# A two-layer decoder trunk on one core: the two passes with high weights as one matmul of 512 columns

## The chip, the core and the metric

The kernel runs on one core of a Trainium2 chip. The metric is the device time of one execution in microseconds; before the change it is 662.47 us (median of 3 runs, 661.54 to 662.65). The core's engines are TensorE (PE in the rows, its weight loads PEld), VectorE (DVE), ScalarE (ACT), GpSimd (POOL) and SyncE (SP, which issues most of the transfers here). TensorE writes into PSUM, eight banks of 128 partitions x 512 fp32.

## The reference, cut to what matters

```python
def reference(x, ...):                       # x: (1, 256, 1024) float32
    for i in range(2):
        h = rms_norm(x, norm_mix_g[i])
        x = x + (nsa_mixer(h, ...) if i == 0 else diff_mixer(h, ...))
        h = rms_norm(x, norm_ffn_g[i])
        x = x + conv_ffn(h, ...)
    return rms_norm(x, final_norm_g)

def rms_norm(x, g):
    return x * lax.rsqrt(jnp.mean(x * x, axis=-1, keepdims=True) + EPS) * g

def diff_mixer(h, w_in, ...):
    q, k, v = split(h @ w_in)                # 8 heads, two halves of 64 each
    p = softmax(q k / 8 - slopes * dist)     # of each half, causal
    a = p[:, 0] - lam * p[:, 1]
    return (rms_norm(a @ v, subln_g) * (1.0 - lambda_init)) @ w_out

def conv_ffn(h, w_up, conv_w, conv_b, w_down):
    u = causal_conv3(h @ w_up) + conv_b      # per channel, 2 x 2816 channels
    gate, val = jnp.split(u, 2, axis=-1)
    return (jax.nn.silu(gate) * val) @ w_down
```

The first mixer (`nsa_mixer`, 16 heads, three branches of attention) is touched by the change in its output projection alone.

## The kernel before

x lies transposed in `xT`: 8 tiles of 128 channels x 256 tokens. To keep fp32 accuracy, each product runs as three matmul passes on rounded parts: the weights as `hi` and `lo`, the activations as `xhi` and `xlo`, and the passes are hi by xhi, hi by xlo and lo by xhi (`passes`, L220). With the weights stationary (`mm_b`, L224), a pass over one tile is a matmul of 128x128 weights by 256 columns, so a unit of weights (128x1024, 8 tiles) takes 8 x 3 = 24 matmuls.

The class `Stream` (L60 on) brings the weights in the order of use: SyncE issues the transfers into three raw buffers, ScalarE makes `hi` of a unit (L112), VectorE `lo` (L113). `fill` keeps some units ahead.

The norm is applied late. `split_tile` (L182) splits x times gain, without the factor of a token, as soon as a residual tile is there; `norm_stats` (L201) sums the squares by TensorE, takes the power on GpSimd, makes a diagonal `dg` on VectorE (L212), spreads it by TensorE and copies it (L217) into `rr`, the factor of each token. The results of the projections are multiplied by `rr` when they leave PSUM: L762 in the diff mixer, L960 in the feed-forward.

The four phases run as `nsa`, `ffn(0)`, `diff`, `ffn(1)`. TensorE's order is that of the program text (a manual schedule for this engine); the order of VectorE, ScalarE and GpSimd is made by the scheduler of the language from dependencies and priorities. PSUM banks come from one pool of 8 in the order of their requests.

In the feed-forward a pair p (of 22) is one unit of gate channels and one of value channels. `up(p)` (L941) does 48 matmuls into one bank, gate in its first 256 columns and value in the last. `conv(p)` (L957) takes the bank by one multiply with `rr` into `us` (VectorE, L960), then the convolution (ScalarE L965, VectorE L967 four times), silu, product, and the split into `hh` (ScalarE, L974) and `hl` (VectorE, L976). `down(p - 2)` follows up(p) on TensorE: 24 matmuls of 256 columns in layer 0 (L932), 12 of 512 in layer 1 (L912). The second layer also puts `rows(i)`, four transposes (L988), behind the pairs 3, 5, 7 and 9.

`residual` (L262) adds a bank of an output projection to `xT`, splits the tile and adds its squares to the sum. In the diff mixer `proj(h, w)` makes q and k of a head (24 matmuls), `s_scores` the scores and both softmax halves (scaled and combined at L782 and L783), `s_trans` transposes them and copies them to `dva` (L794), `s_pv` multiplies them by V (L801). Its V projection (L244) takes x as the stationary side and 512 columns of weights.

Of the kernel before, what the change touches and what calls it, by code (L numbers as in the profile page):

```python
# [10 lines left out]
F32 = mybir.dt.float32  # L11
F32R = mybir.dt.float32r
# [5 lines left out]
P = 128  # L18
T = 256
# [10 lines left out]
LOOK = 3  # L30
GW = 280
# [94 lines left out]
def trunk(ctx, tc, xin, wts, cst, kst, sel, bia, msk, bib, lam, fng, out):  # L126
# [35 lines left out]
    xhi = cp.tile([P, KT, T], F32R, name="xhi")  # L162
    xlo = cp.tile([P, KT, T], F32R, name="xlo")
# [77 lines left out]

    def mm_a1(dst, unit, cols, k, kt, q):
# [19 lines left out]
    def residual(n, st, dt, ps):  # L262
        nc.vector.tensor_tensor(xT[:, dt, :], ps, xT[:, dt, :], op=OP.add)  # L263
        split_tile(n, dt)
        sum_squares(n, st, square(n, dt)[:, 0, :], dt)

    def nsa():
        with ExitStack() as c2:
# [266 lines left out]
            oh = ohp.tile([P, 2 * KT * T], F32R, tag="sh", name="oh")  # L535
            ohi = oh[:, : KT * T].rearrange("p (k t) -> p k t", k=KT)
            olo = oh[:, KT * T :].rearrange("p (k t) -> p k t", k=KT)
# [122 lines left out]
            def oproj(dt, k0, k1):  # L660
# [3 lines left out]
                mm_b(ps[:, :T], u, ohi, olo, k0, k1)  # L664
                if k1 == KT:
                    residual(1, st, dt, ps[:, :T])
# [50 lines left out]
    def diff(st):  # L717
        with ExitStack() as c2:
# [6 lines left out]
            oh = ohp.tile([P, 2 * KT * T], F32R, tag="sh", name="doh")  # L725
            ohi = oh[:, : KT * T].rearrange("p (k t) -> p k t", k=KT)
            olo = oh[:, KT * T :].rearrange("p (k t) -> p k t", k=KT)
# [27 lines left out]
            def proj(h, w, k0, k1):  # L755
# [3 lines left out]
                mm_b(ps[:, :T], u, xhi, xlo, k0, k1)  # L759
                if k1 == KT:  # L760
                    t = at.tile([P, T], F32, tag=f"qk{w}", name=f"dqks{h}{w}", bufs=3)
                    nc.vector.tensor_tensor(t, ps[:, :T], (rneg, rr)[w], op=OP.mult)  # L762
                    qk[h, w] = t

            def s_scores(h):
# [15 lines left out]
                for q, (a, b) in enumerate(((0, P), (P, 384))):  # L781
                    nc.vector.tensor_scalar(pt[:, 1, a:b], pt[:, 1, a:b], ls[:, 1, q : q + 1], None, op0=OP.mult)  # L782
# [48 lines left out]
            def oproj(dt, k0, k1):  # L831
# [3 lines left out]
                mm_b(ps[:, :T], u, ohi, olo, k0, k1)  # L835
                if k1 == KT:
                    residual(3, st, dt, ps[:, :T])
# [44 lines left out]
    def ffn(l, st, oproj_rest, dt0):  # L882
        with ExitStack() as c2:
# [57 lines left out]
            def up(p, k0=0, k1=KT):  # L941
                if k0 == 0:
                    ups[p] = ((S.next(), S.next()), bank(f"u{l}{p}").rearrange("p (a t) -> p a t", a=2))
                units, ps = ups[p]
                for kt in range(k0, k1):
                    for b in range(2):
                        for i, (w, x) in enumerate(passes(units[b], xhi, xlo)):
                            nc.tensor.matmul(  # L948
                                ps[:, b, :],
                                w[:, kt * P : (kt + 1) * P],  # L950
                                x[:, kt, :],
# [256 lines left out]
```

## Time and profile before

| | |
|---|---|
| time, median of 3 runs | 662.47 us (661.54 to 662.65) |
| the profiled execution | 662.05 us, of which the span 660.3 us |
| TensorE busy | 639.2 us, 97% of the span |
| VectorE busy | 513.9 us, 78% |
| ScalarE busy | 415.0 us, 63% |
| GpSimd busy | 28.5 us, 4% |
| read from memory | 109.27 MB, 167 GB/s over the span |
| chain that ended last | TensorE 67% of the span, of it L948 (up) 35%, L932 and L912 (down) 10% and 9%, L233 of q and k 6% |

The page gives busy time per engine, then tenths of busy time in 40 slices of the span, then the chain of work that ended last. Busy times of matmuls overlap (one of 256 columns lasts some 280 ns from its start to its modelled end, while the next starts long before), so a pace is read from a row of matmuls in the chain, as length by count, and not from the mean of one. The same holds for short operations of VectorE in a row.

### The profile page before, as it was taken

How to read it: one execution, taken by the hardware profiler on the slowest of the kernel's cores; microseconds unless marked ns; L12 is line 12 of the kernel's file. 1: busy time of each engine (PE TensorE's matmuls, PEld its weight loads, DVE VectorE, ACT ScalarE, POOL GpSimd, SP SyncE). 2: the span in 40 equal slices, each digit the busy share in tenths (PEclk: the TensorE clock that was granted, in tenths of full speed). 3: DMA queues.
4: the chain of work that ended last, by engine and by line, in shares of the span. 5: the costliest groups of instructions: out<-in, count | busy, mean ns of one | idle time of the engine just before them, and what ended most of it. 6: DMA issues, size and time to landing. Idle time of an engine off the chain costs nothing.

```text
span 660.3 us, 12584 instructions
## 1 busy us (share of the span) xinstructions
PE 639.2 (97%) x5026; PEld 609.3 (92%) x5026; DVE 513.9 (78%) x990; ACT 415.0 (63%) x817; POOL 28.5 (4%) x40
## 2 busy tenths in 40 slices
PE   8999999999999999999999999999999999999994
PEld 7989888889999999999998998989999999999993
DVE  6999988759967777788858589855987777779674
ACT  7797988658655555566636477645666555558342
POOL 3200000000000000000002000000100000000002
PEclk9999999999999999999999999999999999999998
DMA  8977301125455555555714555621755555555301
GB/s 301 308 269 267 136 16 60 65 97 201 182 193 192 192 191 188 174 184 190 255 65 148 195 159 208 216 96 31 293 188 192 192 192 188 185 180 179 99 1 64
DMA packets 15770, 111.12 MB, mean 168 GB/s; under 512 B 1976, under 2 KB 3512, under 8 KB 5976
## 3 DMA queue, kind: packets, MB, share of 16 engines
q1 hardware_dynamic: 15120, 109.70, 46.8%
q0 software_dynamic: 448, 0.37, 0.5%
q8 instruction: 39, 0.64, 0.4%
q10 hardware_dynamic: 144, 0.26, 0.1%
q14 instruction: 19, 0.16, 0.1%
HBM read 109.27 MB, written 1.05 MB: 167 GB/s over the span
## 4 chain that ended last, share of the span: by engine, by line
PE 67%; issue 23%; DVE 5%; ACT 2%; POOL 1%; DMA 1%; SPq 0%; POOLq 0%; DVEq 0%; ACTq 0%
PE u L948 35%; PE acc L932 10%; PE acc L912 9%; PE dqk L233 6%; PE dv L244 3%; PE dop L233 2%; DVE lo L113 1%; ACT dp L260 1%; DMA xT<-xin 1%; DVE cv L967 0%; PE ds L776 0%; PE ds L775 0%; DVE xT L263 0%; PE dta L792 0%; ACT xhi L183 0%
## 5 line engine op out<-in xcount | busy, mean ns | idle before, releaser
L112 ACT CAST hi<-raw 128x1024 fp32r<-128x1024 f32 (+2 forms) x199 | 202.5, 1044 | 103.5 <-PE u L948 55.4
L113 DVE TENSOR_TENSOR lo<-raw,hi 128x1024 fp32r<-128x1024 f32 (+2 forms) x199 | 239.3, 1222 | 16.1 <-ACT hi L112 15.5
L948 PE MATMUL u<-xlo,hi 128*128 128x256 f32 x704 | 197.7, 281 | 0.9 <-DVE xlo L184 0.9
L948 PE MATMUL u<-xhi,lo 128*128 128x256 f32 x704 | 198.6, 282 | 0.0
L948 PE MATMUL u<-xhi,hi 128*128 128x256 f32 x704 | 198.5, 282 | 0.0
L948 PEld LDWEIGHTS u<-xlo,hi 128*128 128x128 f32 x704 | 132.7, 188 | 1.8 <-DVE xlo L184 1.1
L948 PEld LDWEIGHTS u<-xhi,hi 128*128 128x128 f32 x704 | 132.7, 189 | 0.8 <-ACT xhi L183 0.2
L948 PEld LDWEIGHTS u<-xhi,lo 128*128 128x128 f32 x704 | 132.5, 188 | 0.0
L967 DVE SCALAR_TENSOR_TENSOR cv<-us,cs,cv 128x255 f32<-128x255 f32 (+1 forms) x176 | 74.5, 478 | 4.2 <-ACT cv L965 3.7
L960 DVE TENSOR_TENSOR us<-u,rrs 128x512 f32<-128x512 f32 x44 | 30.3, 690 | 53.3 <-PE u L948 53.2
L965 ACT ACTIVATE cv<-us,cs 128x256 f32<-128x256 f32 x88 | 48.1, 593 | 13.4 <-DVE us L960 13.2
L932 PE MATMUL acc<-hl,hi 128*128 128x256 f32 x176 | 49.7, 283 | 1.0 <-DVE hl L976 1.0
L932 PE MATMUL acc<-hh,lo 128*128 128x256 f32 x176 | 49.7, 282 | 0.0
L932 PE MATMUL acc<-hh,hi 128*128 128x256 f32 x176 | 49.6, 282 | 0.0
L974 ACT CAST hh<-cv 128x256 fp32r<-128x256 f32 x44 | 17.8, 405 | 44.6 <-DVE cv L972 44.6
L233 PE MATMUL dqk<-xhi,hi 128*128 128x256 f32 x128 | 37.1, 290 | 0.0
L233 PE MATMUL dqk<-xhi,lo 128*128 128x256 f32 x128 | 36.0, 281 | 0.0
L233 PE MATMUL dqk<-xlo,hi 128*128 128x256 f32 x128 | 36.0, 281 | 0.0
L932 PEld LDWEIGHTS acc<-hl,hi 128*128 128x128 f32 x176 | 33.2, 189 | 1.2 <-DVE hl L976 1.2
L932 PEld LDWEIGHTS acc<-hh,hi 128*128 128x128 f32 x176 | 33.3, 189 | 0.0
L932 PEld LDWEIGHTS acc<-hh,lo 128*128 128x128 f32 x176 | 33.2, 189 | 0.0
L976 DVE TENSOR_TENSOR hl<-cv,hh 128x256 fp32r<-128x256 f32 x44 | 18.6, 424 | 16.1 <-ACT hh L974 16.1
(243 smaller groups left out, 1258.7 us busy)
## 6 DMA issues: line engine op xcount, KB each, us to landing
raw<-wts SPq DMA_DIRECT2D x40, 1536.0 KB, 6.7
raw<-wts SPq DMA_DIRECT2D x34, 1024.0 KB, 5.0
raw<-wts SPq DMA_DIRECT2D x7, 512.0 KB, 4.7
raw<-wts SPq DMA_DIRECT2D x2, 1120.0 KB, 7.5
db<-bib SPq DMA_DIRECT2D x8, 192.0 KB, 4.1
xT<-xin SPq DMA_DIRECT2D x4, 256.0 KB, 5.1
out<-z SPq DMA_DIRECT2D x3, 256.0 KB, 2.0
raw<-wts SPq DMA_DIRECT2D x2, 256.0 KB, 4.5
```

The lines of the kernel that those rows point to most:

```text
L112: nc.scalar.copy(hi[:, q], r[:, q])
L113: nc.vector.tensor_tensor(lo[:, q], r[:, q], hi[:, q].bitcast(F32), op=OP.subtract)
L233: nc.tensor.matmul(dst, w[:, kt * P : (kt + 1) * P], x[:, kt, :], start=kt == 0 and i == 0, stop=kt == KT - 1 and i == 2, skip_group_check ...
L244: nc.tensor.matmul(dst, x[:, kt, q * P : (q + 1) * P], w[:, k * cols : (k + 1) * cols], start=kt == 0 and i == 0, stop=kt == KT - 1 and i ...
L912: nc.tensor.matmul(acc[q][c // 512][:, c % 512 : c % 512 + d - c], x[:, qs], w[:, c:d], start=p == 0 and i == 0, stop=p == NPAIR - 1 and i ...
L932: nc.tensor.matmul(acc[dt // 2][:, dt % 2, :], w[:, dt * P : (dt + 1) * P], x, start=p == 0 and i == 0 and dt % 2 == 0, stop=p == NPAIR - ...
L948: nc.tensor.matmul(ps[:, b, :], w[:, kt * P : (kt + 1) * P], x[:, kt, :], start=kt == 0 and b == 0 and i == 0, stop=kt == KT - 1 and i == ...
L960: nc.vector.tensor_tensor(us, ps, rr.unsqueeze(1).to_broadcast([P, 2, T]), op=OP.mult)
L965: nc.scalar.activation(cv[:, b, :], us[:, b, :], AF.Identity, bias=w[3], scale=w[2])
L967: nc.vector.scalar_tensor_tensor(cv[:, b, sft:], us[:, b, : T - sft], w[2 - sft], cv[:, b, sft:], op0=OP.mult, op1=OP.add)
L974: nc.scalar.copy(hh, h)
L976: nc.vector.tensor_tensor(hl, h, hh.bitcast(F32), op=OP.subtract)
```

## The change

`xhi` and `xlo` become the two halves of one tile `xs`, side by side for each of the 8 tiles of x. `mm_w` does the two passes with `hi` as one matmul of 512 columns ([xhi | xlo]) and the pass with `lo` as one of 256 columns into the second half of the bank. The result is the sum of the two halves of the bank. It is used for all up projections, for q and k of the diff mixer, and for the output tiles 0 to 5 of both output projections, whose input `oh` is laid out in the same way.

Each user now adds the halves: a copy of the second half on ScalarE and an add on VectorE (up and q, k), or two adds to `xT` (residual). An up pair takes two banks, and it runs tile by tile over both units only for the pairs 0, 3 and 4, unit by unit otherwise. After up(3) `normalize()` writes `xs` anew, multiplied by `rr`, so that from pair 4 on no multiply is needed at the exit. In the diff mixer the scaling of the second softmax half goes from VectorE to ScalarE.

```diff
+NORM = 4
-    xhi = cp.tile([P, KT, T], F32R, name="xhi")
-    xlo = cp.tile([P, KT, T], F32R, name="xlo")
+    xs = cp.tile([P, KT, 2, T], F32R, name="xs")
+    xhi, xlo = xs[:, :, 0, :], xs[:, :, 1, :]
...
+    def mm_w(ps, unit, x, k0=0, k1=KT):
+        hi, lo = unit
+        for kt in range(k0, k1):
+            ws = slice(kt * P, (kt + 1) * P)
+            nc.tensor.matmul(
+                ps, hi[:, ws], x[:, kt].rearrange("p s t -> p (s t)"), start=kt == 0, stop=False, skip_group_check=True
+            )
+            nc.tensor.matmul(ps[:, T:], lo[:, ws], x[:, kt, 0, :], start=False, stop=kt == KT - 1, skip_group_check=True)
...
-    def residual(n, st, dt, ps):
-        nc.vector.tensor_tensor(xT[:, dt, :], ps, xT[:, dt, :], op=OP.add)
+    def residual(n, st, dt, *ps):
+        for part in ps:
+            nc.vector.tensor_tensor(xT[:, dt, :], part, xT[:, dt, :], op=OP.add)
...
-                mm_b(ps[:, :T], u, ohi, olo, k0, k1)
+                if dt < 6:
+                    mm_w(ps, u, oh, k0, k1)
+                else:
+                    mm_b(ps[:, :T], u, ohi, olo, k0, k1)
                 if k1 == KT:
-                    residual(3, st, dt, ps[:, :T])
+                    residual(3, st, dt, *[ps[:, i * T : i * T + T] for i in range(1 + (dt < 6))])
...
-                mm_b(ps[:, :T], u, xhi, xlo, k0, k1)
+                mm_w(ps, u, xs, k0, k1)
                 if k1 == KT:
                     t = at.tile([P, T], F32, tag=f"qk{w}", name=f"dqks{h}{w}", bufs=3)
-                    nc.vector.tensor_tensor(t, ps[:, :T], (rneg, rr)[w], op=OP.mult)
+                    nc.scalar.copy(t, ps[:, T:])
+                    nc.vector.tensor_tensor(t, ps[:, :T], t, op=OP.add)
+                    nc.vector.tensor_tensor(t, t, (rneg, rr)[w], op=OP.mult)
...
-                    nc.vector.tensor_scalar(pt[:, 1, a:b], pt[:, 1, a:b], ls[:, 1, q : q + 1], None, op0=OP.mult)
+                    nc.scalar.activation(pt[:, 1, a:b], pt[:, 1, a:b], AF.Copy, scale=ls[:, 1, q : q + 1])
...
             def up(p, k0=0, k1=KT):
                 if k0 == 0:
-                    ups[p] = ((S.next(), S.next()), bank(f"u{l}{p}").rearrange("p (a t) -> p a t", a=2))
+                    ups[p] = ((S.next(), S.next()), [bank(f"u{l}{p}{b}") for b in range(2)])
                 units, ps = ups[p]
-                for kt in range(k0, k1):
+                if p in (0, NORM - 1, NORM):
+                    for kt in range(k0, k1):
+                        for b in range(2):
+                            mm_w(ps[b], units[b], xs, kt, kt + 1)
+                else:
                     for b in range(2):
...
+                        mm_w(ps[b], units[b], xs, k0, k1)
+
+            def normalize():
+                for kt in range(KT):
+                    t = wk.tile([P, 1, T], F32, tag="sq", name=f"xn{l}{kt}", bufs=2)[:, 0, :]
+                    nc.vector.scalar_tensor_tensor(t, xT[:, kt, :], gain(2 * l + 1, kt), rr, op0=OP.mult, op1=OP.mult)
+                    nc.scalar.copy(xhi[:, kt, :], t)
+                    nc.vector.tensor_tensor(xlo[:, kt, :], t, xhi[:, kt, :].bitcast(F32), op=OP.subtract)
...
-                nc.vector.tensor_tensor(us, ps, rr.unsqueeze(1).to_broadcast([P, 2, T]), op=OP.mult)
+                for b in range(2):
+                    nc.scalar.copy(us[:, b, :], ps[b][:, T:])
+                    nc.vector.tensor_tensor(us[:, b, :], ps[b][:, :T], us[:, b, :], op=OP.add)
+                if p < NORM:
+                    nc.vector.tensor_tensor(us, us, rr.unsqueeze(1).to_broadcast([P, 2, T]), op=OP.mult)
...
                 up(p)
+                if p == NORM - 1:
+                    normalize()
                 conv(p)
```

TensorE in the second feed-forward, from the end of down(1) into up(4), before (`hi144` and `hi145` are the two units of pair 4, `u14` their bank):

```order
L912 MATMUL acc111_6107<-hi143_6124,hl11_6028 128x512
L988 MATMUL xr0_6210<-ks__71,xT_73 128x128 x4
L948 MATMUL u14_6230<-xhi_97,hi144_6130 128x256
L948 MATMUL u14_6230<-xlo_98,hi144_6130 128x256
L948 MATMUL u14_6230<-xhi_97,lo144_6131 128x256
L948 MATMUL u14_6230<-xhi_97,hi145_6216 128x256
L948 MATMUL u14_6230<-xlo_98,hi145_6216 128x256
L948 MATMUL u14_6230<-xhi_97,lo145_6217 128x256
```

The same place after (`u140` and `u141` are the two banks):

```order
L929 MATMUL acc111_5665<-hi143_5682,hl11_5597 128x512
L1012 MATMUL xr0_5789<-ks__71,xT_73 128x128 x4
L247 MATMUL u140_5809<-xs_97,hi144_5688 128x512
L250 MATMUL u140_5809<-xs_97,lo144_5689 128x256
L247 MATMUL u141_5810<-xs_97,hi145_5795 128x512
L250 MATMUL u141_5810<-xs_97,lo145_5796 128x256
```

Three matmuls of 256 columns became one of 512 and one of 256, and the pair of units now writes two banks where it wrote one.

VectorE in the second layer, residual tiles 4 and 5 ahead of the second feed-forward, before (L263 adds the bank, L113 splits weights, L184 makes `xlo`, L198 adds squares):

```order
L263 TENSOR_TENSOR xT_73<-dop4_5654,xT_73 128x256
L263 TENSOR_TENSOR xT_73<-dop5_5673,xT_73 128x256
L198 TENSOR_TENSOR ss32_5741<-ss31_5731,sq32_5739 128x256
L113 TENSOR_TENSOR lo135_5790<-raw59_5783,hi135_5789 128x1024
L198 TENSOR_TENSOR ss33_5751<-ss32_5741,sq33_5749 128x256
L184 SCALAR_TENSOR_TENSOR xlo_98<-xT_73,cs_70,xhi_97 128x256
```

The same tiles after (L274, L114, L185 and L199 are the same steps):

```order
L274 TENSOR_TENSOR xT_73<-dop4_5263,xT_73 128x256
L185 SCALAR_TENSOR_TENSOR xs_97<-xT_73,cs_70,xs_97 128x256
L199 TENSOR_TENSOR ss32_5332<-ss31_5322,sq32_5330 128x256
L185 SCALAR_TENSOR_TENSOR xs_97<-xT_73,cs_70,xs_97 128x256
L199 TENSOR_TENSOR ss33_5342<-ss32_5332,sq33_5340 128x256
L274 TENSOR_TENSOR xT_73<-dop4_5263,xT_73 128x256
L274 TENSOR_TENSOR xT_73<-dop5_5276,xT_73 128x256
L114 TENSOR_TENSOR lo135_5381<-raw59_5374,hi135_5380 128x1024
L185 SCALAR_TENSOR_TENSOR xs_97<-xT_73,cs_70,xs_97 128x256
L199 TENSOR_TENSOR ss34_5352<-ss33_5342,sq34_5350 128x256
L274 TENSOR_TENSOR xT_73<-dop5_5276,xT_73 128x256
```

Each residual tile is added in two steps, which stand apart in the row.

VectorE in the second feed-forward, around the exit of pair 3 (`us13`), before:

```order
L976 TENSOR_TENSOR hl12_6102<-cv12_6091,hh12_6100 128x256
L960 TENSOR_TENSOR us13_6183<-u13_6134,rrs3_5974 128x512
L113 TENSOR_TENSOR lo147_6227<-raw64_6224,hi147_6226 128x1024
L113 TENSOR_TENSOR lo148_6307<-raw64_6224,hi148_6306 128x1024
L967 SCALAR_TENSOR_TENSOR cv13_6185<-us13_6183,cs_70,cv13_6185 128x255 x2
```

The same place after (`xn1k` is tile k of x times gain and `rr`, L973 makes it and L975 its low part):

```order
L1000 TENSOR_TENSOR hl12_5660<-cv12_5649,hh12_5658 128x256
L975 TENSOR_TENSOR xs_97<-xn12_5734,xs_97 128x256
L975 TENSOR_TENSOR xs_97<-xn13_5738,xs_97 128x256
L973 SCALAR_TENSOR_TENSOR xn14_5742<-xT_73,cs_70,rrs3_5543 128x256
L973 SCALAR_TENSOR_TENSOR xn15_5746<-xT_73,cs_70,rrs3_5543 128x256
L982 TENSOR_TENSOR us13_5758<-u130_5692,us13_5758 128x256
L982 TENSOR_TENSOR us13_5758<-u131_5693,us13_5758 128x256
L975 TENSOR_TENSOR xs_97<-xn14_5742,xs_97 128x256
L975 TENSOR_TENSOR xs_97<-xn15_5746,xs_97 128x256
L973 SCALAR_TENSOR_TENSOR xn16_5750<-xT_73,cs_70,rrs3_5543 128x256
L973 SCALAR_TENSOR_TENSOR xn17_5754<-xT_73,cs_70,rrs3_5543 128x256
L984 TENSOR_TENSOR us13_5758<-us13_5758,rrs3_5543 128x512
```

Four steps of the normalizing stand between `hl12` and the first add that empties a bank of up(3).

## Rows read from the trace of the kernel before

**Rows 1.** The page: busy time of each engine, and the granted clock in tenths.

```profile
PE 639.2 (97%) x5026; PEld 609.3 (92%) x5026; DVE 513.9 (78%) x990; ACT 415.0 (63%) x817; POOL 28.5 (4%) x40
...
PEclk9999999999999999999999999999999999999998
```

**Rows 2.** Chain of waits, first feed-forward: start us, length us, engine, tile, line, count.

```profile
176.19 3.00 PE acc L932 x23
179.19 5.67 PE u L948 x48
184.86 2.88 PE acc L932 x24
```

**Rows 3.** The same chain, diff mixer and second feed-forward.

```profile
365.10 5.59 PE dv L244 x24
370.69 8.60 PE dqk L233 x72
...
480.73 2.73 PE acc L912 x12
483.46 5.69 PE u L948 x48
```

**Rows 4.** Waits of TensorE: line, releaser, us in total, times, longest us.

```profile
PE do L801 <- ACT dva L794: 2.3, 2, 1.4
...
PE acc L932 <- DVE hl L976: 1.0, 1, 1.0
PE u L948 <- DVE xlo L184: 0.9, 1, 0.9
```

**Rows 5.** Stretches: bounds, us, busy us of each engine (instructions), clock, transfers.

```profile
core 0: us, PE busy (x) PEld busy (x) DVE busy (x) ACT busy (x) POOL busy (x), PEclk, DMA share, GB/s
147.10:187.70 40.60, 39.58 (x332) 39.33 (x331) 35.61 (x63) 28.32 (x48) 1.63 (x1) 1.00 0.53 195
184.80:338.60 153.80, 153.80 (x1299) 153.80 (x1298) 119.67 (x183) 89.99 (x129) 0.00 (x0) 1.00 0.54 191
453.80:492.30 38.50, 37.56 (x291) 36.10 (x290) 34.95 (x63) 28.16 (x47) 1.72 (x1) 1.00 0.60 219
```

**Rows 6.** Timeline of VectorE, start of the first feed-forward: start us, length us.

```profile
156.70 1.07 DVE L263 TENSOR_TENSOR xT<-op,xT 128x256 f32<-128x256 f32 x3
...
161.43 0.48 DVE L184 SCALAR_TENSOR_TENSOR xlo<-xT,cs,xhi 128x256 fp32r<-128x256 f32 x1
...
165.19 0.48 DVE L212 TENSOR_SCALAR dg<-ks__71,rc 128x128 f32<-128x128 f32 x2 [0.62 <-POOL rc L209]
165.59 2.36 DVE L113 TENSOR_TENSOR lo<-raw,hi 128x1024 fp32r<-128x1024 f32 x2
167.86 0.69 DVE L960 TENSOR_TENSOR us<-u,rrs 128x512 f32<-128x512 f32 x1
...
175.71 0.42 DVE L976 TENSOR_TENSOR hl<-cv,hh 128x256 fp32r<-128x256 f32 x1
...
187.78 1.66 DVE L967 SCALAR_TENSOR_TENSOR cv<-us,cs,cv 128x255 f32<-128x255 f32 x4
```

**Rows 7.** Groups of instructions: count, busy us, mean ns, idle us before and its releaser.

```profile
L782 DVE TENSOR_SCALAR dp<-dp,dls 128x128 f32<-128x128 f32 (+1 forms) x16 | 4.4, 316 | 0.2
...
L762 DVE TENSOR_TENSOR dqks<-dqk,drneg 128x256 f32<-128x256 f32 x8 | 3.3, 418 | 1.3 <-PE dqk L233 1.3
...
L217 ACT COPY rrs<-rr 128x256 f32<-128x256 f32 x4 | 1.5, 372 | 5.9 <-PE rr L215 5.9
```

**Rows 8.** Timeline of VectorE, start of the second feed-forward.

```profile
466.37 0.47 DVE L184 SCALAR_TENSOR_TENSOR xlo<-xT,cs,xhi 128x256 fp32r<-128x256 f32 x1
...
470.94 0.48 DVE L212 TENSOR_SCALAR dg<-ks__71,rc 128x128 f32<-128x128 f32 x2 [0.58 <-POOL rc L209]
```

**Rows 9.** Timeline of TensorE, one head of the diff mixer.

```profile
406.19 0.49 PE L801 MATMUL do<-dV,dva 128*128 128x128 f32 x2 [1.36 <-ACT dva L794]
```

More of the change, by code (lines that the diff above doesn't have):

```diff
@@ L533, in nsa @@
             gv = gt.rearrange("p q (h c) -> p q h c", c=3)
-            oh = ohp.tile([P, 2 * KT * T], F32R, tag="sh", name="oh")
-            ohi = oh[:, : KT * T].rearrange("p (k t) -> p k t", k=KT)
-            olo = oh[:, KT * T :].rearrange("p (k t) -> p k t", k=KT)
+            oh = ohp.tile([P, 2 * KT * T], F32R, tag="sh", name="oh").rearrange("p (k s t) -> p k s t", k=KT, s=2)
+            ohi, olo = oh[:, :, 0, :], oh[:, :, 1, :]
             ph_, pairs = {}, {}
@@ L663, in oproj @@
                 ps, u = ops[dt]
-                mm_b(ps[:, :T], u, ohi, olo, k0, k1)
+                if dt < 6:
+                    mm_w(ps, u, oh, k0, k1)
+                else:
+                    mm_b(ps[:, :T], u, ohi, olo, k0, k1)
                 if k1 == KT:
-                    residual(1, st, dt, ps[:, :T])
+                    residual(1, st, dt, *[ps[:, i * T : i * T + T] for i in range(1 + (dt < 6))])
             for k in range(NH // 2):
@@ L942, in up @@
                 if k0 == 0:
-                    ups[p] = ((S.next(), S.next()), bank(f"u{l}{p}").rearrange("p (a t) -> p a t", a=2))
+                    ups[p] = ((S.next(), S.next()), [bank(f"u{l}{p}{b}") for b in range(2)])
                 units, ps = ups[p]
-                for kt in range(k0, k1):
-                    for b in range(2):
[L947 to L951, printed above, removed]
-                                start=kt == 0 and b == 0 and i == 0,
-                                stop=kt == KT - 1 and i == 2,
-                                skip_group_check=True,
-                            )
+                if p in (0, NORM - 1, NORM):
+                    for kt in range(k0, k1):
+                        for b in range(2):
+                            mm_w(ps[b], units[b], xs, kt, kt + 1)
+                else:
+                    for b in range(2):
+                        mm_w(ps[b], units[b], xs, k0, k1)
[5 more added lines that the diff above has]
+                    nc.vector.tensor_tensor(xlo[:, kt, :], t, xhi[:, kt, :].bitcast(F32), op=OP.subtract)
             def conv(p):
```

9 lines of the change are left out of this document (5 added, 4 removed).

## The prediction, made before the changed kernel was run

> **What bounds the kernel now.** The page first. TensorE's line of busy time reads 97% of the span, VectorE's 78%, ScalarE's 63%, and the granted-clock line stays at nine tenths and more [rows 1]. The chain that ended last shows what that means: from 176.19 us on it is one row of matmuls behind the other, 48 of an up projection, 24 of a down projection, with no gap between them (176.19 + 3.00 = 179.19, 179.19 + 5.67 = 184.86), and the same in the second feed-forward, with rows of 12 at L912 [rows 2, 3]. So in most of the kernel a nanosecond per matmul is a nanosecond of the end, and what matters is (a) how fast 512-column matmuls follow one another against 256-column ones, and (b) the few places where TensorE waits for VectorE or ScalarE, since the change gives these engines more to do.
>
> The waits of TensorE that bear on the change are three: L801 for the copy `dva` (2.3 us in all, 1.4 the longest), L932 for `hl` once (1.0), L948 for `xlo` once (0.9) [rows 4]. The last two are the starts of the two feed-forwards. The table by stretches puts prices beside them: VectorE was busy 35.61 of 40.60 us from the residual to the end of up(3) in the first, 34.95 of 38.50 in the second, but 119.67 of 153.80 (78%) in the steady stretch, with ScalarE at 89.99 (59%) and TensorE at 153.80 of 153.80 [rows 5].
>
> **Matmuls: what the merged form saves.** A triple of three 256-column matmuls becomes one of 512 and one of 256. Per 256 columns the rows give 5.67/48 = 118.1 ns (up) to 8.60/72 = 119.4 ns (dqk) [rows 2, 3]. A bare 512-column matmul with its own weights takes 2.73/12 = 227.5 ns (L912) or 5.59/24 = 232.9 ns (dv) [rows 3]. Two of 256 for one of 512 therefore saves between 2 x 118.1 - 232.9 = 3.4 ns and 2 x 119.4 - 227.5 = 11.4 ns. Pairs of the same phase give 2 x 118.5 - 227.5 = 9.5 (up beside L912 of the second feed-forward, 5.69/48) and 2 x 119.4 - 232.9 = 6.0 (dqk beside dv). I take 7, between these two and nearer the smaller, because the new sequence still alternates lengths, which no row shows. Triples: 22 pairs x 2 layers x 16 = 704 in up, 128 in the projections of diff, 96 in the two output projections.
>
> **First feed-forward, start.** The six residual tiles now take two adds instead of one; three such adds took 1.07 us, so 6 more are some 2.04 us at a pace of 0.34 [rows 6]. From 147.1 us VectorE runs nearly without a gap until `dg` (165.19 to 165.67), so `xlo` of the last tile, which ends at 161.9 before, comes at about 163.95, and `dg` at 167.8 instead of 165.67. What the output projection gains (48 x 7 ns) is lost in the wait for `xlo`, here and in the second layer. From `dg` to `hl` of pair 0 (it begins at 175.71) VectorE needed 10.5 us. After, in its new order, there are five adds of 0.34 (us00, us01 and half of us02), two multiplies at 0.6 (one alone takes 0.69), three weight splits at 1.13, six scaled operations at 0.4, and 0.34 and 0.42 for the last product and `hl`: 9.5 us, at the paces that back-to-back rows give [rows 6]. One weight split fewer stands ahead. `hl` is then ready at 177.3 against 176.13, and down(0) starts 1.15 us late. Gains of up(0) to up(2) vanish in that wait.
>
> The 8 normalizing steps (one scaled multiply and one subtract on VectorE, 0.73 us; one cast on ScalarE) follow up(3) in the program, but stand partly earlier in VectorE's order. up(4) takes its tiles one after the other; by the ledger tile 4 is ready at 189.3 and needed at about 191, so nothing is waited for here. From up(3) on TensorE is the bound again, and 19 pairs x 16 x 7 ns = 2.13 us come back. Layer 0: +1.15 - 2.13 = **-0.98**.
>
> **Steady stretch.** Per pair of units VectorE exchanges one 512-wide multiply (0.69) for two adds (about 0.68): nothing. ScalarE gets two copies; the nearest, `rrs`, reads the same shape from a bank in 372 ns [rows 7], so 0.74 in a period of 8.55, 59% to 67%. Weight splits have two periods of room and a bank of up(p) is free about 11 us before up(p+2) wants it. I cost this at nothing; the cover is VectorE's 22% of idle time [rows 5].
>
> **Second feed-forward, start.** The same 2.04 us on VectorE: here the tile before the last, whose `xlo` begins at 466.37, comes at 468.85, up(0) ends 2.1 later, and down(0) starts about 1.5 later (482.25 for 480.73), since part is made up by idle time around `dg` and by up(1) and up(2) [rows 3, 8]. After down(1) come the transposes of `rows(0)`, which take a bank; with two banks for each up, the second bank of up(4) is the one that up(3) used first, and the first matmul into it waits for the add of us13. In VectorE's order that add stands behind the normalizing steps of tiles 2 to 5, where before the multiply of us13 followed `hl` at once. I put it at 495.3 against 494.1 at which TensorE arrives: +1.15. Less 2 x 0.11 for up(3) and up(4), TensorE is +2.4 late at the end of up(4); 17 pairs x 16 x 7 ns = 1.90 follow. Layer 1: **+0.5**.
>
> **Diff mixer.** 128 x 7 ns = -0.90. Its evacuations cost ScalarE a copy (0.37 [rows 7]) and VectorE an add and a multiply for one multiply (0.42 each); the scaling of the second softmax half leaves VectorE (316 ns x 16 = 4.4 us) for ScalarE. In ScalarE's new order the copy `dva` stands ahead of the exponentials that it followed, so the 1.36 us of [rows 9] should shrink; beside it a new short wait for the scores of a head. I take half of the 1.36 back: -0.7; bounds -1.4 and +1.4, nothing gained or one such wait more. Layer: **-1.6**.
>
> Sum: -0.98 + 0.5 - 1.6 = -2.08 us. The profiled run took 662.05, 0.4 below the median 662.47, and no stretch of it is out of the ordinary; the sum goes on the median: 660.4.
>
> **Rivals.** *The low pace.* The merged matmul is worth the 3.4 ns of the dv row and not 7. Then 36 pairs x 16 + 128 triples give back 704 x 3.6 ns = 2.5 us less: 662.9, no change. For it speaks that dv is the bare 512-column form beside ScalarE and VectorE traffic, against it L912, which stands in the very loop. A rule stands beside this rival. The Trainium skill (TensorE: Matmul & The Clock Gate, section on the back-to-back issue gap) gives N/2.4 + 2.5 ns for a matmul of N columns at the full clock, by which two of 256 are 218.4 and one of 512 is 215.8: an estimate of 2.5 ns saved per pair, and 704 x 4.5 ns = 3.2 us less gain, 663.6. The rows, with 118.1 and 227.5, lie 9 and 12 ns above that rule, so it is the rows that decide here.
>
> *The VectorE backlog (slower).* Up to up(4) each feed-forward start gives VectorE 2.04 (residuals) + 4 x 0.68 (adds beside the multiply of pairs 0 to 3) + 8 x 0.73 (normalizing) = 10.6 us more, and it was idle for only 40.60 - 35.61 = 5.0 and 38.50 - 34.95 = 3.5 us there [rows 5]. If up(4) has to wait for the last normalized tiles, TensorE pays the rest: 5.6 + 7.1 = 12.7, of which the sum already holds 1.15 + 2.6; so +8.9, 669.3. It decides when tile 7's `xlo` comes later than up(4) has done tiles 0 to 6. For it: the stretch is tight and the normalizing is all on VectorE; against it: weight splits inside it (1.13 each) can wait two periods, and up(4) eats its tiles in order.
>
> *The scores of diff (slower).* Three steps on two engines now lie between a projection's last matmul and the scores; if ScalarE is inside an exponential of about 0.9 us when the copy comes, each of 7 heads waits that long: +6, 666.4. Against it: before, 1.3 us of idle time stood ahead of that multiply on VectorE in all 8 heads together [rows 7], so the bank was evacuated at once, and a 48-matmul projection lies between.
>
> *The high pace.* 11.4 ns and no wait at L801: 704 x 4.4 ns = 3.1, and 0.5 more of the wait: 656.8.
>
> That the change doesn't do what it says can be excluded: the order of TensorE shows one matmul of 512 and one of 256 columns per tile.
>
> **How the numbers follow.** Forecast 0.41, low pace 0.21, high pace 0.15, VectorE backlog 0.16, diff scores 0.07. The likeliest one's own range is 659.0 to 662.0. A measurement of this kernel can tell about 0.2% from no change, that is 661.15 to 663.8 is "same". Faster: 0.37 of the forecast and the high pace, 0.52. Same: the upper end of the forecast, 0.04, and the low pace, 0.25. Slower: the backlog and the scores, 0.23. The range goes from the high pace's 656.8 to 665.0, which takes in half-sized forms of the two slow cases and leaves out their full size and the far end of the fast one.
>
> **What would show it.** Pace: a row of 32 matmuls of up(p) in the steady stretch should last 16 x (236.3 - 7 + 118.1) ns = 5.56 us for 5.67; below 5.50 is the high pace, above 5.62 the low. The two starts: `hl` of pair 0 as the releaser of L932's first down matmul, 1 to 2 us later than before counted from the residual; a wait of the second bank of up(4) for us13 in layer 1, some 1 us, and none in layer 0. Steady: VectorE still near 78% and TensorE without a gap. Diff: the wait at L801 (of before) below 1 us. I am wrong if TensorE waits for `xs` in up(4) (backlog), if the scores wait at each head, or if a gap opens in the steady stretch for a copy on ScalarE.

## The result

The changed kernel takes 675.09 us (median of 4 runs, 673.6 to 676.82) against 662.56 us for the kernel before (4 runs, 661.54 to 665.76): a ratio of 1.0165, 95% interval 1.0142 to 1.0187. It is slower by 12.5 us, where 660.4 was forecast, and it lies outside the range of 656.8 to 665.0.

The page of the profiled run after (673.76 us, its span 672.0): busy time of each engine and the granted clock in tenths of 40 slices, which answer to [rows 1].

```profile
PE 638.5 (95%) x4098; PEld 565.1 (84%) x4098; DVE 544.7 (81%) x1086; ACT 451.3 (67%) x953; POOL 27.4 (4%) x40
...
PEclk9998999999899999999999999999999999999998
```

TensorE is busy for 0.7 us less than before, and the span is 11.7 us longer, so what grew is idle time; two more slices have the clock digit 8 instead of 9. The waits of TensorE, which answer to [rows 4] (us in total, times, longest):

```profile
PE ds L789 <- DVE dqks L776: 7.2, 6, 2.3
PE u L247 <- DVE xs L185: 6.0, 4, 2.7
PE ph L421 <- ACT hs L417: 3.4, 1, 3.4
...
PE u L247 <- DVE us L982: 0.6, 1, 0.6
...
PE do L815 <- ACT dva L808: 0.2, 1, 0.2
```

The scores of the diff mixer (`ds`) did not wait in the kernel before and now do so six times; the starts of the feed-forwards wait 6.0 us for `xs` where they waited 0.9 for `xlo`; the wait at the copy `dva` is gone, as forecast.

To see where the time went, the span is cut at five rows of the timelines: the first residual add of the first mixer, the first matmul of the V projection, the first matmul of q and k, the first residual add of the diff mixer, and the end. In us, for every kernel of this study:

| kernel | first mixer | first feed-forward | V | diff mixer | second feed-forward to the end | span |
|---|---|---|---|---|---|---|
| before, trace ahead of the prediction | 147.1 | 199.9 | 23.5 | 83.3 | 206.5 | 660.3 |
| before, second trace (e0_before) | 148.6 | 200.0 | 23.5 | 83.3 | 206.5 | 661.9 |
| after | 151.0 | 202.3 | 23.5 | 86.9 | 208.3 | 672.0 |
| e1_late | 148.6 | 199.0 | 23.5 | 83.3 | 204.6 | 659.0 |
| e2_diff_back | 152.3 | 201.9 | 23.5 | 83.6 | 210.4 | 671.7 |
| e3_oproj_back | 152.5 | 197.9 | 23.5 | 87.0 | 205.3 | 666.1 |
| e4_no_norm | 149.6 | 204.4 | 23.5 | 86.8 | 209.5 | 673.8 |
| e5_best | 149.6 | 197.9 | 23.5 | 83.3 | 204.6 | 658.8 |
| e6_twice | 150.9 | 202.2 | 23.5 | 83.3 | 208.7 | 668.6 |
| e7_exits | 149.3 | 197.9 | 23.5 | 93.9 | 204.4 | 668.9 |
| e8_scale | 150.5 | 198.0 | 23.5 | 83.0 | 204.6 | 659.5 |
| e9_by_pass | 152.2 | 197.6 | 23.5 | 83.3 | 205.1 | 661.6 |
| e10_exit_dve | 153.2 | 197.9 | 23.5 | 92.3 | 204.6 | 671.4 |

Of the 11.7 us between the spans before and after, 2.4 lie in the first feed-forward, 3.6 in the diff mixer, 1.8 in the second feed-forward, 7.8 in all. The other 3.9 lie in the first mixer up to its first residual add, where the change touches, besides the layout of x, only the last matmuls, those of the output projection.

### The profile page after: what moved, and what is told of

It is laid out like the page before. It is cut to its first block, busy times and chain, and to the rows that moved or that the text cites. A ratio compares the mean times of both kernels' runs of the same rounds, so it can differ in the third digit from the quotient of the medians.

```text
span 672.0 us, 10973 instructions
## 1 busy us (share of the span) xinstructions
PE 638.5 (95%) x4098; PEld 565.1 (84%) x4098; DVE 544.7 (81%) x1086; ACT 451.3 (67%) x953; POOL 27.4 (4%) x40
## 4 chain that ended last, share of the span: by engine, by line
PE 79%; DVE 10%; ACT 5%; issue 2%; DMA 2%; POOL 1%; SPq 0%; POOLq 0%; ACTq 0%; DVEq 0%
PE u L247 24%; PE u L250 12%; PE acc L949 9%; PE acc L929 8%; PE dv L254 3%; PE q L234 2%; PE o L654 2%; PE dqk L247 2%; DVE lo L114 2%; ACT hi L113 2%; PE kc L234 2%; DVE p L610 1%; PE k L234 1%; PE dop L247 1%; PE op L247 1%
## 5 line engine op out<-in xcount | busy, mean ns | idle before, releaser
L114 DVE TENSOR_TENSOR lo<-raw,hi 128x1024 fp32r<-128x1024 f32 (+2 forms) x199 | 242.4, 1223 | 51.4 <-ACT hi L113 50.3
L113 ACT CAST hi<-raw 128x1024 fp32r<-128x1024 f32 (+2 forms) x199 | 205.1, 1043 | 96.8 <-PE u L247 50.9
L247 PE MATMUL u<-xs,hi 128*128 128x512 f32 x704 | 252.3, 399 | 6.5 <-DVE xs L185 6.0
L250 PE MATMUL u<-xs,lo 128*128 128x256 f32 x704 | 198.2, 281 | 0.3 <-DVE lo L114 0.3
L247 PEld LDWEIGHTS u<-xs,hi 128*128 128x128 f32 x704 | 132.9, 189 | 38.5 <-DVE xs L185 7.3
L250 PEld LDWEIGHTS u<-xs,lo 128*128 128x128 f32 x704 | 133.4, 189 | 1.3 <-DVE lo L114 0.6
L991 DVE SCALAR_TENSOR_TENSOR cv<-us,cs,cv 128x254 f32<-128x254 f32 (+1 forms) x176 | 80.5, 480 | 7.8 <-ACT cv L989 5.5
L247 PE MATMUL dqk<-xs,hi 128*128 128x512 f32 x128 | 46.7, 403 | 0.0
L982 DVE TENSOR_TENSOR us<-u,us 128x256 f32<-128x256 f32 x88 | 36.1, 418 | 4.3 <-ACT us L981 4.2
L250 PE MATMUL dqk<-xs,lo 128*128 128x256 f32 x128 | 35.8, 280 | 0.0
L981 ACT COPY us<-u 128x256 f32<-128x256 f32 x88 | 31.4, 366 | 5.3 <-PE u L250 5.2
L929 PE MATMUL acc<-hi,hh 128*128 128x512 f32 x88 | 28.0, 392 | 0.0
```

The costliest lines, as they stand in the source:

```text
L113: nc.scalar.copy(hi[:, q], r[:, q])
L114: nc.vector.tensor_tensor(lo[:, q], r[:, q], hi[:, q].bitcast(F32), op=OP.subtract)
L247: nc.tensor.matmul(ps, hi[:, ws], x[:, kt].rearrange("p s t -> p (s t)"), start=kt == 0, stop=False, skip_group_check=True)
L250: nc.tensor.matmul(ps[:, T:], lo[:, ws], x[:, kt, 0, :], start=False, stop=kt == KT - 1, skip_group_check=True)
L929: nc.tensor.matmul(acc[q][c // 512][:, c % 512 : c % 512 + d - c], x[:, qs], w[:, c:d], start=p == 0 and i == 0, stop=p == NPAIR - 1 and i ...
L981: nc.scalar.copy(us[:, b, :], ps[b][:, T:])
```

## The experiments

Two theories stood after the result. The first: each stage lost its time to its own edit (double adds and normalizing at the starts, longer exits in the diff mixer), and the first mixer's length is a matter of single executions. The second: the new layout of x delays the first mixer too.

**Only the steady part of the change.**

In the kernel before, with `xhi` and `xlo` as the halves of `xs`:

```diff
...
+                if p < 4:
...                                           # as before
+                else:
+                    ups[p] = ((S.next(), S.next()), [bank(f"u{l}{p}{b}") for b in range(2)])
+                    units, ps = ups[p]
                     for b in range(2):
...
+                        mm_w(ps[b], units[b], xs)
...
+                    for b in range(2):
+                        nc.scalar.copy(us[:, b, :], ps[b][:, T:])
+                        nc.vector.tensor_tensor(us[:, b, :], ps[b][:, :T], us[:, b, :], op=OP.add)
+                    nc.vector.tensor_tensor(us, us, rb, op=OP.mult)   # rb: rr of both halves
```

> The kernel before with xhi and xlo in one tile and the merged matmul in up for the pairs 4 to 21 alone (copy, add and multiply at their exit, nothing normalized); residual, q and k, scaling in the diff mixer as before. Theory 1 (each stage of the changed kernel lost its time to its own edit, and the later first residual add, 151.0 for 147.1 us, is a matter of single executions): first residual add near 147, starts of the feed-forwards as before (29.1 and 26.9 us from the first residual add to the first down matmul), 36 pairs x 16 x 3.4 ns = 2.0 us gained: 660.5. Theory 2 (the layout of x delays the first mixer): first residual add near 151, 664.4. If VectorE at some 86% can't keep up in the steady stretch: gaps of TensorE there, over 663.

Measured: 662.87 us against 664.92, ratio 0.9964 (0.9944 to 0.9984). The stages are as in theory 1: 0.9 and 1.9 us gained in the two feed-forwards, nothing lost. The time of 660.5 in the expectation stood against the median of the first comparison; against its own runs of before the gain is 2.05 us, as expected. The first residual add came at 148.6, between the two theories' values.

**The diff mixer's edits undone.**

```diff
-                mm_w(ps, u, xs, k0, k1)
+                mm_b(ps[:, :T], u, xhi, xlo, k0, k1)
...
-                    nc.scalar.copy(t, ps[:, T:])
-                    nc.vector.tensor_tensor(t, ps[:, :T], t, op=OP.add)
-                    nc.vector.tensor_tensor(t, t, (rneg, rr)[w], op=OP.mult)
+                    nc.vector.tensor_tensor(t, ps[:, :T], (rneg, rr)[w], op=OP.mult)
```

(and the scaling back on VectorE)

> The changed kernel with q, k and the scaling of the second softmax half as in the kernel before. Theory 1: the waits of the scores (7.2 us in the changed kernel) go, the diff mixer (first dqk matmul to first residual add) takes 83.1 us again for 86.7, and 0.4 us of pace is lost: 671.5. Theory 2 says the same of this stage. If the mixer stays near 86, its loss comes from the weights or from ScalarE's casts, not from this edit: 675.

Measured: 669.94 us, ratio 1.0073 (1.0039 to 1.0106) to before. The diff mixer takes 83.6 us, so its whole loss was in these edits.

**The output projections undone, and the normalizing left out.**

```diff
-                if dt < 6:
+                if dt < 0:
...
-                    residual(3, st, dt, *[ps[:, i * T : i * T + T] for i in range(1 + (dt < 6))])
+                    residual(3, st, dt, *[ps[:, i * T : i * T + T] for i in range(1)])
```

> The changed kernel with both output projections in 256-column matmuls and one add per residual tile. If the double adds cause the late starts: from the first residual add to the first down matmul 30.0 us (for 32.5) in the first layer, with no half-clock stretch there, and 27.5 (for 29.5) in the second: about 670. If the normalizing does: both stay, 674.5.

```diff
-                if p == NORM - 1:
-                    normalize()
...
-                if p < NORM:
+                if p < NPAIR:
                     nc.vector.tensor_tensor(us, us, rr.unsqueeze(1).to_broadcast([P, 2, T]), op=OP.mult)
```

> The changed kernel without the normalizing step; all 22 pairs are multiplied by rr at their exit. If the double adds cause the late starts: 32 and 29 us from the first residual add to the first down matmul, only the wait in up(4) of the second layer (0.7 us) goes: 674. If the normalizing does: 30 and 27.5 us: 670. The multiply adds 0.6 us per pair to VectorE, which in the steady stretch should cost nothing.

Measured: e3_oproj_back 667.79 us, ratio 1.0048 (1.0023 to 1.0074); e4_no_norm 674.74, ratio 1.0133 (1.0095 to 1.0171). With single adds both starts are as before and better than expected: from the first residual add to the first down matmul 27.84 us (after 32.37, before 27.78) and 26.75 (after 29.36, before 26.76). Without the normalizing they stayed late, 34.5 and 31.6, and even later than in the changed kernel, for a reason that the last section comes to. So the output projections hold the late starts. e3_oproj_back undoes their merged matmuls and their double adds together; e6_twice below parts the two. What the normalizing costs is seen beside e5_best, whose second feed-forward is 0.7 us shorter than that of e3_oproj_back: the wait in up(4) of the second layer, and nothing in the first.

**What is left, as a kernel of its own.** The two starts and the diff mixer as before, the merged matmuls in all 22 pairs, a multiply at each exit:

> The changed kernel with the output projections, q, k and the softmax scaling as before and without the normalizing step: merged matmuls in all up projections, a copy, two adds and a multiply at each exit. If the two starts and the diff mixer hold the whole loss: the first feed-forward (first residual add to its end) 197.9 us for 199.9, the second 195.2 for 197.1, the diff mixer 83.3 as before, so 3.9 us faster than before, ratio 0.994. If the multiply at every exit is too much for VectorE: gaps in the steady stretch and no gain.

Measured: 661.0 us (8 runs) against 665.72 (13 runs), ratio 0.994 (0.992 to 0.996). Every stage came out as worked out. This version beats both kernels, the one before by 0.6%. Half of the 2.0 us that it gains in the first feed-forward is the wait of 1.0 us for `hl` [rows 4], which its trace no longer has; the pace of the matmuls gives the other half. Its waits of TensorE and its steady stretch, 18 periods of the first feed-forward (bounds, us, busy us of PE, PEld, DVE, ACT, POOL, clock, transfers):

```profile
PE do L813 <- ACT dva L806: 2.3, 2, 1.4
PE u L247 <- DVE xs L185: 1.4, 1, 1.4
```

```profile
186.20:339.00 152.80, 152.80 (x1011) 139.77 (x1010) 133.23 (x221) 99.44 (x166) 0.00 (x0) 1.00 0.53 192
```

VectorE is busy for 133.2 of 152.8 us (87%), and TensorE has no gap.

**Two adds and nothing else.** The bank of the tiles 0 to 5 is added twice, in the kernel before:

```diff
-        nc.vector.tensor_tensor(xT[:, dt, :], ps, xT[:, dt, :], op=OP.add)
+        for _ in range(1 + (dt < 6)):
+            nc.vector.tensor_tensor(xT[:, dt, :], ps, xT[:, dt, :], op=OP.add)
```

> The kernel before with the bank of the output tiles 0 to 5 added to x twice (so x is not the reference's); no matmul is changed. If the second add by itself delays the feed-forwards: the first takes 203 us and the second 199.5 from the first residual add to its end, for 199.9 and 197.1 (2.0 us of adds each and what follows from them). If it is the merged matmuls or the banks of the output projection: both stay within 0.5 us of before.

Measured, one run (670.37 us): the feed-forwards are 2.3 and 2.2 us longer, 202.2 and 208.7 for 199.9 and 206.5, with no matmul changed; somewhat less than the 3 and 2.4 expected. The first down matmul comes 30.05 and 29.14 us after the first residual add, 2.3 and 2.4 later than before. The waits at the starts (both layers together):

```profile
PE u L949 <- DVE xlo L184: 2.3, 4, 0.9
PE u L949 <- ACT xhi L183: 2.1, 2, 1.5
```

So the bare second adds cost 2.3 and 2.4 us at the two starts.

**Which part of the diff mixer's edits.** From e5_best, the merged q and k with their exits alone, then the scaling alone, then both with the copy on VectorE:

```diff
+                mm_w(ps, u, xs, k0, k1)                           # e7_exits, e10_exit_dve
...
+                    nc.scalar.copy(t, ps[:, T:])                      # e7_exits; e10_exit_dve: nc.vector.tensor_copy
+                    nc.vector.tensor_tensor(t, ps[:, :T], t, op=OP.add)
...
+                    nc.scalar.activation(pt[:, 1, a:b], pt[:, 1, a:b], AF.Copy, scale=ls[:, 1, q : q + 1])   # e8_scale, e10_exit_dve
```

> As e5_best, but with the merged q and k of the changed kernel (copy on ScalarE, add and multiply on VectorE at the exit); the scaling of the softmax half stays on VectorE. If the longer exits make the scores wait: the diff mixer 86.5 us or more, six waits of the scores with 7 us in sum. If the scaling on ScalarE does it: 83.0, since 0.4 us of pace is gained.

> As e5_best, but with the scaling of the second softmax half on ScalarE and nothing else changed in the diff mixer. If the exits make the scores wait: 83.3 us, and the wait for dva at most as before (1.4 us). If the scaling on ScalarE does it: 86 or more.

> The diff mixer of the changed kernel (merged q and k, scaling of the softmax half on ScalarE) in e5_best, with the copy of the second half on VectorE in place of ScalarE. If the copy waits behind weight casts on ScalarE and this is what holds the scores: their waits fall from 7.2 to 3 us or less, diff mixer 84. If VectorE's own queue holds them: 7 us or more, 87 or more.

Measured, one run each: the diff mixer takes 93.9 us with the exits and the scaling on VectorE, 83.0 with the scaling on ScalarE alone, and 92.3 with both and the copy on VectorE. In the first and the last the granted clock also fell to 0.50 behind two of the waits, which took 3.4 us of full clock (the sum of 1 minus the granted clock over stretches of 2 us); in the changed kernel it did not fall in this stage. So the waits are the better measure. Those of the scores, in the first and the last, and that for `dva` in the second:

```profile
PE ds L789 <- DVE dqks L776: 10.3, 8, 3.1
```

```profile
PE ds L789 <- DVE dqks L776: 9.9, 6, 2.6
```

```profile
PE do L813 <- ACT dva L806: 2.6, 2, 1.5
```

The exits make the scores wait, and with the scaling on ScalarE they wait less (7.2 us in the changed kernel against 10.3). Taking the copy off ScalarE made it worse, so the queue that holds them is VectorE's. The changed kernel's own trace agrees: at each of its six waits the copy had ended 0.9 to 1.1 us before VectorE began the add. The wait for `dva` is no shorter with the scaling on ScalarE alone, and with the exits alone (e7_exits) TensorE has none there. The rows of the changed kernel at one wait of the scores show how it comes about. VectorE, then TensorE:

```profile
406.83 1.21 DVE L114 TENSOR_TENSOR lo<-raw,hi 128x1024 fp32r<-128x1024 f32 x1
407.97 0.41 DVE L775 TENSOR_TENSOR dqks<-dqk,dqks 128x256 f32<-128x256 f32 x1
408.30 1.21 DVE L114 TENSOR_TENSOR lo<-raw,hi 128x1024 fp32r<-128x1024 f32 x1
409.43 0.42 DVE L776 TENSOR_TENSOR dqks<-dqks,rrs 128x256 f32<-128x256 f32 x1
```

```profile
409.90 0.50 PE L789 MATMUL ds<-dqks,dqks 64*128 64x128 f32 x4 [1.82 <-DVE dqks L776]
```

The exit was one multiply. It is now an add and a multiply that needs the add, and the scheduler has put a weight split of 1.21 us ahead of the add and another between the two. The multiply that TensorE waits for comes behind both. A split stands between the add and the multiply at five of the six waits. It moves the multiply by some 1.1 us, so it accounts for at most 4.9 of the 7.2 us (an estimate, each of the five waits counted up to 1.13 us). A version in which no split stands between them was not run, so what its removal would give back is not shown.

**Does the order of the lengths set the pace?**

```diff
         for kt in range(k0, k1):
             ws = slice(kt * P, (kt + 1) * P)
             nc.tensor.matmul(ps, hi[:, ws], x[:, kt] ...)       # 512 columns
+        for kt in range(k0, k1):
+            ws = slice(kt * P, (kt + 1) * P)
             nc.tensor.matmul(ps[:, T:], lo[:, ws], x[:, kt, 0, :] ...)   # 256 columns
```

> As e5_best, but the merged matmuls of a unit first all with 512 columns and then all with 256 (pairs 1, 2 and from 5 on). If a 512-column matmul costs 233 ns because the lengths alternate, a row of eight falls to about 227.5 ns each and a pair of units by 16 x 5 = 0.09 us: the 18 periods of the first feed-forward's steady stretch from 152.8 to 151.2 us. If it is its own pace there: no change.

Measured, one run: the same 18 periods last 152.74 us. Below them, one unit of up in the new order.

```profile
188.56:341.30 152.74, 152.74 (x1010) 139.73 (x1010) 134.63 (x220) 98.66 (x166) 0.00 (x0) 1.00 0.54 195
```

```profile
199.74 2.03 PE L247 MATMUL u<-xs,hi 128*128 128x512 f32 x8
201.60 1.12 PE L252 MATMUL u<-xs,lo 128*128 128x256 f32 x8
```

No change against the 152.80 of e5_best, and a row of eight takes (201.60 - 199.74) / 8 = 232.5 ns for each. The pace of the 512-column matmul in up is its own and not one of the alternation.

**The kernel before once more.**

> The kernel before, unchanged, for a second trace of it. If the first mixer's length is a matter of single executions: first residual add anywhere between 147 and 152.5 us, as in the traces of the other kernels, and every later stretch within 0.1 us of the first trace. If the layout of x delays it: 147.1 again.

Measured: the first residual add at 148.6 us, every later stretch within 0.1 us of the first trace. VectorE's row, and the wait of the first mixer that varies from trace to trace:

```profile
148.60 1.50 DVE L263 TENSOR_TENSOR xT<-op,xT 128x256 f32<-128x256 f32 x4 [0.60 <-PE op L233]
```

```profile
PE ph L410 <- ACT hs L406: 1.9, 1, 1.9
```

Over the traces that row is 147.1, 148.6 and 150.9 us with the old layout (before twice, e6_twice) and 148.6 to 153.2 with the new one. The gain of e5_best (new layout) is 2.7 to 5.3 us by its interval, and its later stages give 3.9, so the second theory has nothing for it. That the layout costs up to about a microsecond there is not excluded.

## Why the prediction was wrong, point by point

The forecast and the two profiled runs by stage, in us against the kernel before:

| stage | forecast | measured |
|---|---|---|
| first feed-forward | -0.98 | +2.4 |
| diff mixer | -1.6 | +3.6 |
| second feed-forward | +0.5 | +1.8 |
| first mixer | not in the sum | +3.9 |

The step that failed worst is in the diff mixer: the longer exit of q and k was given one short wait of the scores inside a term of -0.7 us, and TensorE waited six times, 7.2 us in sum. Next comes the start of the first feed-forward, where the 2.04 us of second adds were to shrink to 1.15 us at `hl`: TensorE waited for `xs` instead and lost 1.7 us of full clock behind that. The pace of the merged matmul was half of the forecast in one layer.

**The pace of the merged matmul: right in one layer, half in the other.** The forecast took 7 ns per triple between 3.4 and 11.4. The steady stretch after, the answer to the middle line of [rows 5]:

```profile
192.10:344.88 152.78, 152.78 (x1010) 139.76 (x1010) 129.28 (x215) 100.84 (x173) 0.00 (x0) 1.00 0.55 197
```

The same 18 periods took 153.76 us before (184.86 to 338.62): 0.98 us less, 0.98 / (18 x 16) = 3.4 ns per triple, the end of the bounds that the row of dv gave and the size of the low-pace rival; the 5.63 us of an up projection (below) lie above the 5.62 that the forecast set as its sign. In the second layer it is more. 15 periods there, before and after:

```profile
498.07:626.32 128.25, 128.25 (x913) 120.79 (x913) 98.66 (x152) 75.66 (x111) 0.00 (x0) 1.00 0.50 176
```

```profile
511.19:637.96 126.77, 126.77 (x674) 108.40 (x673) 105.52 (x174) 84.14 (x145) 0.00 (x0) 1.00 0.51 183
```

1.48 us less, 6.2 ns per triple, close to the 7 taken. An up projection after lasts the same in both layers (5.63 us between its first matmul and the next down, a mean over 18 and 15 of them), but before it was 5.68 in the first and 5.74 in the second, so it was the 256-column form that differed. In the second layer every second up projection before was longer:

```profile
552.87 5.69 PE u L948 x48
561.29 5.76 PE u L948 x48
```

The forecast read one saving for both layers from the one row of 5.69 in [rows 3] and the 5.67 of [rows 2]; the longer form was in neither, and why it is longer is not shown. So the 7 ns fit the second layer by luck. L912 was the wrong price for a 512-column matmul of up, which costs 233 ns in either order (e9_by_pass), as in dv. The term was 1.1 us too large for the first layer (19 x 16 x 3.6 ns) and close in the second. The formula of the Trainium skill (TensorE: Matmul & The Clock Gate, back-to-back issue gap), which the page gives for a matmul by itself, makes 2.5 ns of this difference, below both measured values; its 218 and 216 ns are below the rows' 236 and 233, so the rows decide.

**Steady stretch: right in time.** TensorE has no gap, and ScalarE rose to 66% where 67% was said. VectorE is at 85% (129.28 of 152.78) where 78% was said to stay; 4.4 us of this are the last steps of the normalizing and of pair 3, which fall into the stretch, and without them it is 82%.

**First feed-forward, start: the term was there, its path and size were not.** The 2.04 us of second adds are right (2.3 in e6_twice). What the sum left out stands behind them. ScalarE, VectorE and TensorE at that place of the changed kernel:

```profile
164.14 0.71 ACT L191 ACTIVATE sq<-xT 128x256 f32<-128x256 f32 x2
166.86 1.04 ACT L113 CAST hi<-raw 128x1024 fp32r<-128x1024 f32 x1 [2.01 <-DMA raw<-wts]
167.81 0.50 ACT L184 ACTIVATE xs<-xT,cs 128x256 fp32r<-128x256 f32 x1
```

```profile
168.35 0.48 DVE L185 SCALAR_TENSOR_TENSOR xs<-xT,cs,xs 128x256 fp32r<-128x256 f32 x1 [0.67 <-ACT xs L184]
```

```profile
165.20 0.50 PE L247 MATMUL u<-xs,hi 128*128 128x512 f32 x1 [0.74 <-DVE xs L185]
168.88 0.50 PE L247 MATMUL u<-xs,hi 128*128 128x512 f32 x1 [1.94 <-DVE xs L185]
```

On ScalarE a weight cast stands ahead of the cast of the last tile of x and waits 2.01 us for its transfer, which was issued late (at 159.69) because its raw buffer was freed late by a split on VectorE (158.41 to 159.6). VectorE, free again, waits 0.67 us for that cast. So the wait of 1.94 us on TensorE is the adds and a queue behind them. Then the clock falls. Stretches of 1 to 2 us (bounds, us, busy us of PE, PEld, DVE, ACT, POOL, granted clock, transfers):

```profile
168.90:170.00 1.10, 1.10 (x8) 1.01 (x8) 1.10 (x2) 0.58 (x1) 0.00 (x0) 1.00 0.08 34
...
171.00:172.00 1.00, 1.00 (x5) 0.90 (x4) 0.52 (x1) 0.96 (x2) 1.00 (x1) 0.50 1.01 184
172.00:173.00 1.00, 1.00 (x5) 0.80 (x4) 0.86 (x4) 0.00 (x0) 0.11 (x1) 0.50 0.80 283
...
174.00:176.00 2.00, 2.00 (x13) 1.74 (x12) 0.90 (x2) 0.37 (x1) 0.00 (x0) 1.00 0.83 344
```

At a granted clock of 0.50 (the 1.2 GHz level) the pairs of matmuls follow every 0.64 us (they start at 171.19, 171.82 and 172.47) and not every 0.35. From 170 to 174 the granted clock was 0.70, 0.50, 0.50 and 0.59, that is 1.7 us of full clock lost. The first down matmul comes 4.6 us later, counted from the residual; 2.3 of it are the adds, 1.7 the clock, and 0.6 is left for the transfer's wait. Some of it came back, since the wait of 1.0 us for `hl` behind that matmul is gone, and 19 pairs gained 1.0: net +2.4 where -0.98 was forecast. The forecast had the delay pass through `hl`, at 1.15 us, and named a later `hl` as the sign to look for. No wait for `hl` remains: the delay passed through `xs`, and nothing absorbed it there.

**Second feed-forward, start: right in kind.** The waits for `xs` in up(0) are

```profile
475.74 0.50 PE L247 MATMUL u<-xs,hi 128*128 128x512 f32 x1 [0.60 <-DVE xs L185]
479.40 0.51 PE L247 MATMUL u<-xs,hi 128*128 128x512 f32 x1 [2.70 <-DVE xs L185]
```

and the first down matmul came 2.6 us later where 1.5 was forecast; the adds alone give 2.4 (e6_twice), so little of them was made up by idle time, as the forecast had it. The wait of up(4)'s second bank for the add of us13 is there, 0.6 us for 1.15. The whole part: +1.8 where +0.5 was forecast, and the pace has no part in the difference.

**Diff mixer: the rival that came was held unlikely, by a misread row.** The forecast said -1.6, the scores rival 6 us more at a chance of 0.07; the stage is 3.6 us longer. The argument against the rival took 1.3 us of idle time ahead of the multiply [rows 7] for a bank that is emptied at once. That row holds the 8 exits of q alone, and little idle time says the reverse: VectorE was mostly busy up to the exit. Over all 16 exits of the kernel before:

```profile
its engine sat idle before it (us, times) until:
  PE dqk L233: 2.8, 4
```

The four times are the first two heads. From then on the multiply of k stood in VectorE's queue. The last matmul into a bank of k before, its multiply, and the scores that need it:

```profile
422.08 0.28 PE L233 MATMUL dqk<-xhi,lo 128*128 128x256 f32 x1
```

```profile
424.96 0.42 DVE L762 TENSOR_TENSOR dqks<-dqk,rrs 128x256 f32<-128x256 f32 x1
```

```profile
427.23 0.50 PE L775 MATMUL ds<-dqks,dqks 64*128 64x128 f32 x4
```

The multiply began 2.6 us after the bank was full (2.6 to 3.9 us in the six later heads), and 1.85 us were left from its end to the scores. With two dependent operations the scheduler has room for a weight split between them, and it used it; the 1.85 us were gone. The rival's mechanism was put on the wrong engine: it is VectorE's queue and not an exponential on ScalarE that holds the exit (the six copies that had ended in time, e10_exit_dve).

The gain at `dva` came (2.3 us of waits to 0.2), but not for the reason given. With the scaling alone on ScalarE that wait stayed (2.6 us in e8_scale), and with the exits alone it was gone (e7_exits); it goes where TensorE is already held up at the scores. That this term came out right is luck. One slip in the working changes nothing: 316 ns x 16 are 5.1 us, and the 4.4 us are busy time with the overlap taken out.

**The VectorE backlog** at up(4) did not come: the normalizing cost 0.7 us in the second layer and nothing in the first.

**What the sum did not speak of.** 3.9 us of the difference between the two profiled runs lie in the first mixer. TensorE waited there 3.4 us for `hs` (1.6 before), and the granted clock from 50 to 55 us was 0.97, 0.50, 0.50, 0.50 and 0.82, where it did not fall before: 1.8 us of wait and 1.7 of full clock. The same wait lasts 1.6, 1.9 and 3.2 us in the three traces with the old layout and 1.8 to 4.3 in the ten with the new, and the clock lost behind it is 0 to 3.4 us in both, so this is not shown to be the change's. What makes `hs` late was not followed up. How much of the 12.5 us between the medians of the first comparison comes from it, with four runs on each side, stays open; the stages alone give 7.8. In later rounds the kernel before had medians of 664.92 (21 runs) and 665.72 us (13 runs), so that 12.5 is more likely too large than too small.

## What to carry to other kernels

Merging two 256-column matmuls into one of 512 was worth 3.4 to 6.2 ns here, 1 to 2% of a triple, so it pays only where what must then be added at the exit is hidden entirely: in a long steady stretch it was (e5_best, 0.6% for the kernel with the lost wait for `hl`), at the start of a stage and in front of short dependent steps it was not. Before an exit is made longer, look at what else stands in that engine's queue, and read little idle time ahead of the exit as a full queue: a second dependent operation gives a scheduler a place for a long one. And when a start gets later, price not the added operations alone but also the transfers that are issued later behind them and the clock that can fall in or behind a wait of TensorE.

## What the runs showed of the hardware

That a wait can cost more than its length was not in the forecast. The granted clock fell to 0.50 after the 1.94 us wait above and, in the second trace of the kernel before, after its 1.9 us wait in the first mixer (46.00 to 52.00):

```profile
46.00:48.00 2.00, 1.28 (x7) 1.28 (x8) 1.94 (x3) 1.98 (x5) 0.00 (x0) 0.77 0.38 57
48.00:50.00 2.00, 2.00 (x12) 2.00 (x10) 1.48 (x2) 0.49 (x2) 0.00 (x0) 0.50 0.83 336
50.00:52.00 2.00, 2.00 (x17) 2.00 (x17) 1.70 (x6) 1.90 (x4) 0.00 (x0) 0.88 1.00 324
```

In the first trace, after 1.63 us at the same place, it did not fall. Nor is it the same each time: with the 2.70 us wait at the start of the second feed-forward it did not fall in the changed kernel, but it did with the same wait in e2_diff_back (475 to 483 us, 0.57, 0.50, 0.50, 0.72) and in e4_no_norm. Before the last output, each fall in the traces of this study cost 1.7 or 3.4 us of full clock (the sum of 1 minus the granted clock over stretches of 1 us). At the starts of the feed-forwards e4_no_norm lost 3.4 us twice, the changed kernel 1.7 and nothing, and its starts are 2.2 us later each. Mean granted clocks of the runs of the changed kernel lie between 0.983 and 0.990, its profiled run at 0.990; the profiled run of the kernel before is at 0.997, 21 runs of it in a later round between 0.990 and 0.997.
